# A two-layer mixer on one core: inputs and parameters laid out transposed, and the first modulation's depth tiles spread over the column groups

## The chip, the core and the metric

The kernel runs on one core of a Trainium2 chip. TensorE (PE) does the matrix products, VectorE (DVE) and ScalarE (ACT) the elementwise work, GpSimd (POOL) a few small powers, and SyncE (SP) issues all DMAs. The metric is the device time of one execution in microseconds. Three runs before the change took 1480.5 to 1486.15 us, median 1482.35.

## What is computed

Two layers of a mixer over 256 context tokens and 256 latent tokens, 2048 channels. What matters here, cut from the reference:

```python
def _modulation(cvec, ada_w, ada_b):
    m = jax.nn.silu(cvec) @ ada_w + ada_b      # (2048,) @ (2048, 3 * 2048)
    return jnp.split(m, 3, axis=-1)            # shift, scale, gate

def _layer(x, ctx, c, c_ctx, lp, cos, sin, update_ctx):
    sh_x, sc_x, g_x = [m[:, None, :] for m in _modulation(c, lp["ada_w"], lp["ada_b"])]
    sh_c, sc_c, g_c = _modulation(c_ctx, lp["ada_w"], lp["ada_b"])
    hx = rmsnorm(x, lp["pre_g"]) * (1.0 + sc_x) + sh_x
    hc = rmsnorm(ctx, lp["pre_g"]) * (1.0 + sc_c) + sh_c
    px = hx @ lp["w_in"]
    if update_ctx:
        pc = hc @ lp["w_in"]
    ...
    o_x = lax.map(lambda qs: _attend(qs[0], qs[1], k_nope, k_rope, v), ...)
    x_new = x + g_x * _branch_merge(o_x, px, lp)   # attention and long convolution, gated,
    ...                                            # normalised, times w_out
```

All is in float32. No projection of the first layer can start before its rows of `hx` are there, and these need the norm of x and the shift and scale of their channels, which need a (2 x 2048) by (2048 x 128) product for each tile of 128 channels.

## The kernel before

Activations lie with channels on the partitions: a tile is 128 channels by 512 tokens (256 of context, 256 latent), and the 16 tiles over the 2048 channels are "depth tiles". A float32 product is made of three passes with operands split into a high and a low part (`mm3`, two fp32r halves made by a ScalarE cast and a VectorE subtraction); the modulation matmuls alone run in plain float32, and each shows as two records in the trace.

The program is written by a list scheduler in Python (`Net`). Jobs yield operations; `run` issues, of those that could start first by its own estimate of every engine's queue (`start_of`, with the costs in `mm`, `act`, `dot` and so on), the one of the lowest rank. So the costs decide how jobs are interleaved on each engine. On top of that stands a fixed list of weight items (`items`, rank 10 on TensorE): `loader` loads them in order, `prepper` splits them, `products` multiplies them in order, each waiting for the names in its `need`. Buffers come from pools: slots of 256 KB (`s`), five of 512 KB (`raw`), two of 512 KB for high parts (`hi`). The loader takes raws when they are free and otherwise pairs of slots, if at least `SPARE_RAW` slots are to spare and the item is within `LOAD_DEPTH` of the current one.

The first stage goes so. `setup` and `load_x` load c, small tensors and x with tokens on partitions; `first_norm` transposes x on TensorE (64 transposes of 128x128, copied out of PSUM), squares it and makes the row factors. `params` transposes the per-channel parameters. Then come the blocks of channel tiles, `BLOCKS`: two of 2 tiles and three of 4. For a block, `ada_first` multiplies silu(c) (32 columns of `cs`, two of them used) by the scale columns and by the shift columns of the block. Each of the block's tiles has its own group of 32 columns of the array and accumulates over all 16 depth tiles:

```python
for c in range(n):                              # n = 2 or 4 tiles of the block
    o = (j * n + c) * P
    yield self.mm(ps[32 * c:32 * c + 32, 0:P], self.cs[:, kt, :], raws[0][:, o:o + P],
                  kt == 0, kt == KT - 1, ...)
```

`ada_cols` copies the sum, transposes it once and adds the bias; `hx_job` modulates the block's tiles of x; the projections' early items (`early`, seven groups, cut by depth into parts named `late`) use them. The list holds a block's modulation items, and from the ninth on (`EARLY_FROM`) the projection items of the block before between them. The first six projection items of the first block use two depth tiles only and are finished later (`by_depth`). The last four tiles of the shift are made on VectorE by dot products (`ada_slow`, `WAVE2`). After the first stage follow the other projections, attention heads, the long convolution and the output product of the first layer, then the second layer.

Names in the rows: `in_p_ada_first` are the first modulation's weights, `in_p_win` the input projection's, `cs` silu(c), `acc` and `mis` PSUM tiles (`acc` for items of the list, `mis` for everything else), `mcol` and `acol` shift and scale by channel. All matmuls are recorded at L232, transposes at L235, DMAs at L309, ScalarE's at L243 and L245, most of VectorE's at L250.

Of the kernel before, what the change touches and what calls it, by code (L numbers as in the profile page):

```python
# [9 lines left out]
F32 = mybir.dt.float32  # L10
# [23 lines left out]
N_SLOTS = 96 - 2 * (N_RAW + N_HI)  # L34
# [14 lines left out]
WAVE2 = (((0, 0, 12, 16),), ("ada0_0_4",), 4)  # L49
# [18 lines left out]
N_EARLY = 3  # L68
EARLY_FROM = 8
# [4 lines left out]
N_ROWS_A = sum(n for _, n in PARAM_ROWS)  # L74
N_ROWS_B = 96
# [94 lines left out]
class Net:  # L170
# [107 lines left out]
    def dot(self, junk, a, b, acc):  # L278
        return Op("dve", 0.07 + free_size(a) * 0.00104, [junk, acc], [a, b],
# [220 lines left out]
    def setup(self):  # L500
        nc, a, c = self.nc, self.a, self.const
        self.crow = c.tile([2 * KT, P], F32, name="crow")
        self.do(self.dma(self.crow, a["p_c"]))
        self.ident = c.tile([P, P], F32, name="ident")
        self.do(self.dma(self.ident, a["k_ident"]))
# [12 lines left out]
    def late_setup(self):  # L518
        a, c = self.a, self.const
        self.rows_a = self.slots.get()  # L520
        self.rows_b = self.slots.get()
        self.do(self.dma(self.rows_a[0:N_ROWS_A, 0:2 * P], a["p_rows_a"]))
        self.do(self.dma(self.rows_b[0:N_ROWS_B, 0:2 * P], a["p_rows_b"]))
# [4 lines left out]
    def cond(self):  # L528
        yield from self.on(self.crow, self.ident)
        (ps,) = yield from self.pget()  # L530
# [3 lines left out]
        self.mis.put(ps)  # L534
# [6 lines left out]
    def params(self):  # L541
        c = self.const
        self.par = []
        for l in range(2):
# [4 lines left out]
            d["col"] = c.tile([P, 224], F32, name=f"col_{l}")  # L549
            n = 0  # L550
            for k, m in PARAM_ROWS:
                d[k] = d["col"][:, n:n + m]
# [1283 lines left out]
```

## Time and profile before

| | |
|---|---|
| median of 3 runs | 1482.35 us (1480.5 to 1486.15) |
| span of the profiled execution | 1483.1 us |
| busy: PE, DVE, ACT | 98%, 80%, 47% |
| DMA | 328.92 MB, mean 222 GB/s |
| granted TensorE clock, mean | 0.995 |

The span runs from the first to the last instruction of one profiled execution. Busy times are shares of that span. A busy TensorE is not TensorE at its peak: records overlap, so throughput is read from the distance between starts or from the length of a row divided by its count, not from the mean duration of one.

### The profile page before, as it was taken

The page shows a single profiled execution, that of the slowest core. Times are in us where ns is not written, and L with a number is a line of the kernel's source. Part 1 is how long each engine was busy: PE and PEld are TensorE (multiplying, and loading weights), DVE is VectorE, ACT ScalarE, POOL GpSimd, SP SyncE. Part 2 cuts the span into 40 slices and gives each one's busy share as a digit, 9 for nine tenths or more (in the row PEclk, how much of TensorE's full clock was granted, in tenths as well). Part 3 has the DMA queues.
Part 4 walks back from the last instruction along what each step waited for, and adds up shares of the span by engine and source line. Part 5 has one row for each costly group of instructions (what it writes and reads, how often), then busy time and mean ns, then how long its engine had stood idle before and what let it go on. Part 6 is the DMA issues. An engine that isn't in the chain of part 4 may idle for free.

```text
span 1483.1 us, 26318 instructions
## 1 busy us (share of the span) xinstructions
PE 1457.0 (98%) x9700; PEld 1261.2 (85%) x9700; DVE 1190.2 (80%) x2522; ACT 692.6 (47%) x1339; POOL 16.4 (1%) x20
## 2 busy tenths in 40 slices
PE   7999999999999999999999999999999999999997
PEld 5677787778787777877778999999999989999997
DVE  5577999997888878998888988888868878786544
ACT  5421354335354452334334444566646666655542
POOL 0000000000000000000000000000000000000000
PEclk9999999999999999999999999999999999999999
DMA  9997875468466677566858886567728234668441
GB/s 324 356 334 239 286 263 205 159 212 308 151 195 215 223 250 251 170 228 220 299 191 301 296 281 196 167 227 260 245 89 310 90 113 133 234 201 288 164 143 57
DMA packets 165872, 328.92 MB, mean 222 GB/s; under 512 B 18501, under 2 KB 41068, under 8 KB 165744
## 3 DMA queue, kind: packets, MB, share of 16 engines
q1 hardware_dynamic: 165744, 327.25, 64.6%
q8 instruction: 76, 1.25, 0.3%
q14 instruction: 52, 0.43, 0.1%
HBM read 301.99 MB, written 25.18 MB: 221 GB/s over the span
## 4 chain that ended last, share of the span: by engine, by line
PE 88%; DMA 7%; DVE 2%; issue 1%; SPq 1%; ACT 1%; POOL 0%; DVEq 0%; POOLq 0%; ACTq 0%
PE acc L232 68%; PE mis L232 17%; PE mis L235 3%; DMA s<-in_p_ada_first 1%; DMA raw<-in_p_ada_first 1%; DMA s<-in_p_ada_slow 1%; DVE s L250 1%; DMA s<-in_p_win 1%; SPq L309 1%; DMA s<-in_ctx 1%; DVE junk L280 1%; DMA s<-in_p_uv 0%; DMA raw<-in_p_win 0%; DMA s<-in_p_ada_rest 0%; DMA h_d<-s 0%
## 5 line engine op out<-in xcount | busy, mean ns | idle before, releaser
L232 PE MATMUL acc<-s,hi 128*128 128x256 f32 (+1 forms) x2304 | 566.0, 337 | 0.5 <-ACT hi L243 0.4
L232 PE MATMUL acc<-s,s 128*128 128x256 f32 (+1 forms) x3216 | 489.4, 308 | 0.0
L232 PEld LDWEIGHTS acc<-s,s 128*128 128x128 f32 x3216 | 439.2, 191 | 30.5 <-issue 3.7
L232 PEld LDWEIGHTS acc<-s,hi 128*128 128x128 f32 x2304 | 388.4, 191 | 56.2 <-issue 11.5
L250 DVE TENSOR_TENSOR s<-s,s 128x512 fp32r<-128x512 f32 (+5 forms) x575 | 342.2, 623 | 42.3 <-ACT s L245 21.2
L232 PE MATMUL acc<-s,raw 128*128 128x256 f32 (+1 forms) x1104 | 371.1, 336 | 0.3 <-DVE raw L250 0.3
L280 DVE SCALAR_TENSOR_TENSOR junk<-s,s 128x512 bf16<-128x512 f32 x352 | 241.5, 686 | 26.9 <-DMA s<-crow_d 10.5
L232 PE MATMUL mis<-s,s 128*128 128x256 f32 (+2 forms) x1232 | 251.4, 341 | 1.2 <-ACT s L243 0.9
L232 PEld LDWEIGHTS acc<-s,raw 128*128 128x128 f32 x1104 | 210.3, 191 | 23.0 <-issue 2.5
L232 PEld LDWEIGHTS mis<-s,s 128*128 128x128 f32 (+1 forms) x1232 | 190.4, 189 | 43.9 <-issue 13.9
L243 ACT CAST s<-s 128x512 fp32r<-128x512 f32 (+3 forms) x324 | 180.3, 589 | 74.8 <-DVE s L250 28.5
L243 ACT CAST hi<-raw 128x1024 fp32r<-128x1024 f32 (+1 forms) x100 | 97.2, 972 | 121.4 <-PE acc L232 68.7
L250 DVE TENSOR_TENSOR raw<-raw,hi 128x1024 fp32r<-128x1024 f32 x88 | 107.3, 1220 | 19.7 <-ACT hi L243 19.1
L243 ACT CAST hi<-s 128x512 fp32r<-128x512 f32 x124 | 73.4, 618 | 92.9 <-PE acc L232 75.6
L250 DVE TENSOR_TENSOR raw<-s,hi 128x512 fp32r<-128x512 f32 x124 | 83.8, 686 | 34.4 <-ACT hi L243 33.4
L243 ACT COPY s<-mis 128x512 f32<-128x512 f32 (+3 forms) x101 | 48.6, 485 | 116.7 <-PE mis L232 90.5
L250 DVE TENSOR_TENSOR s<-mis,s 128x512 fp32r<-128x512 f32 (+2 forms) x128 | 84.6, 669 | 22.8 <-ACT s L243 17.3
L243 ACT CAST s<-mis 128x512 fp32r<-128x512 f32 (+1 forms) x100 | 56.6, 570 | 89.2 <-PE mis L235 48.3
L245 ACT ACTIVATE s<-acc 128x256 f32<-128x256 f32 (+1 forms) x88 | 37.5, 429 | 96.6 <-PE acc L232 81.2
L235 PE MATMUL mis<-ident,s 128*128 128x128 f32 (+1 forms) x369 | 66.8, 291 | 4.1 <-DMA s<-in_x 1.0
L250 DVE TENSOR_TENSOR s<-raw,s 128x512 fp32r<-128x512 f32 x106 | 69.8, 683 | 0.8 <-ACT s L243 0.7
L243 ACT CAST s<-raw 128x512 fp32r<-128x512 f32 x106 | 61.8, 617 | 9.1 <-DMA raw<-in_p_wout 6.2
(85 smaller groups left out, 916.9 us busy)
## 6 DMA issues: line engine op xcount, KB each, us to landing
s<-in_p_ada_slow SPq DMA_DIRECT2D x208, 256.0 KB, 3.3
raw<-in_p_win SPq DMA_DIRECT2D x99, 512.0 KB, 5.1
s<-in_p_win SPq DMA_DIRECT2D x178, 256.0 KB, 5.3
s<-in_p_wout SPq DMA_DIRECT2D x108, 256.0 KB, 4.9
raw<-in_p_wout SPq DMA_DIRECT2D x42, 512.0 KB, 3.8
s<-in_p_ada_first SPq DMA_DIRECT2D x62, 256.0 KB, 5.8
raw<-in_p_ada_first SPq DMA_DIRECT2D x25, 512.0 KB, 6.1
raw<-in_p_ada_rest SPq DMA_DIRECT2D x20, 512.0 KB, 4.7
```

The lines of the kernel that those rows point to most:

```text
L232: lambda: self.nc.tensor.matmul(out, lhsT, rhs, start=start, stop=stop), 0.2)
L235: return Op("pe", 0.11, [out], [in_], lambda: self.nc.tensor.transpose(out, in_, ident), 0.2)
L243: self.nc.scalar.copy(out, in_)
L245: self.nc.scalar.activation(out, in_, func, **kw)
L250: return Op("dve", fixed + n * rate, [out], ins, lambda: getattr(self.nc.vector, name)(out=out, **kw))
L280: lambda: self.nc.vector.scalar_tensor_tensor(out=junk, in0=a, scalar=1.0, in1=b, op0=ALU.mult, op1=ALU.mult, accum_out=acc))
L309: return Op("sp", n / 360e3, [dst], [src], lambda: self.nc.sync.dma_start(dst, src))
```

## The change

x and the context come in already transposed, as 16 tiles of 128 channels by 512 tokens, and so do c and the per-channel parameters; the transposes on TensorE, the copies and a DRAM copy of the transposed x go. The first norm squares tiles on ScalarE, adds them on VectorE and sums over the partitions by four small matmuls. In the first modulation, each group of 32 columns now takes every fourth depth tile and all columns of the block (256 or 512) at once; `ada_sum` copies the four partial sums, transposes them and adds them. An item is now 1 MB. The list of the first items is blended evenly: projections of the block before go between the modulation items from the first one. There are seven more slots, four early groups instead of three of the convolution's, a further reserve in the loader, and other costs in the scheduler.

```diff
-N_SLOTS = 96 - 2 * (N_RAW + N_HI)
+N_SLOTS = 103 - 2 * (N_RAW + N_HI)
-WAVE2 = (((0, 0, 12, 16),), ("ada0_0_4",), 4)
+WAVE2 = (((0, 0, 12, 16),), ("ada0_0_2",), 4)
-N_EARLY = 3
-EARLY_FROM = 8
+N_EARLY = 4
...
     def mm(self, out, lhsT, rhs, start=True, stop=True, share=1.0):
-            c = max(n, 480 if n < 256 else 0) / 2400 + 0.0025
+            c = max(n, 480 if n < 256 else 0) / 2400 + 0.0137
-            c = 4 * (n / 2400 + 0.0025) * share if n > 1 else 0.11
+            c = 4 * (n / 2400 + 0.003) * share if n > 1 else 0.11
     def dot(self, junk, a, b, acc):
-        return Op("dve", 0.07 + free_size(a) * 0.00104, [junk, acc], [a, b],
+        return Op("dve", 0.185 + free_size(a) * 0.00104, [junk, acc], [a, b],
+    def promised(self):
+        return max((k.want for k in self.pending if k.name.startswith("mod0")), default=0)
...
     def cond(self):
-        yield self.tr(ps[:, 0:32], self.crow, self.ident[0:32, 0:32])
-        for s in range(2):
-            yield self.act(self.cs[:, :, s], ps[:, s * KT:(s + 1) * KT], AF.Silu)
+        yield self.act(self.cs[:, :, 0:2], self.ccol.rearrange("p (k s) -> p k s", s=2), AF.Silu)
...
     def ada_first(self, sec, t0, t1):
-        n = t1 - t0
-        deep = 8 // n
-        for i in range(2 * n):
+        n = (t1 - t0) * P
+        deep = 2048 // n
+        for i in range(KT // deep):
             def load(raws, i=i):
-                yield from self.load(raws[0], self.a["p_ada_first"][sec, 2 * t0 + i])
+                for h in range(2):
+                    yield from self.load(raws[h], self.a["p_ada_first"][sec, 2 * t0 + 2 * i + h])
             def pe(raws, i=i):
                 for j in range(deep):
-                    kt = deep * i + j
-                    for c in range(n):
-                        o = (j * n + c) * P
-                        yield self.mm(ps[32 * c:32 * c + 32, 0:P], self.cs[:, kt, :], raws[0][:, o:o + P],
-                                      kt == 0, kt == KT - 1, share=0.34 if n == 4 else 0.55)
+                    kt, c = deep * i + j, j % 4
+                    h, o = divmod(j * n, 1024)
+                    yield self.mm(ps[32 * c:32 * c + 32, 0:n], self.cs[:, kt, :], raws[h][:, o:o + n],
+                                  kt < 4, kt >= KT - 4, share=0.37)
+    def ada_sum(self, l, sec, acc, t0, t1):
+        yield self.act(g[:, 0:n], acc[:, 0:n])
+        for i in range(t1 - t0):
+            yield self.tr(ps[:, i * P:(i + 1) * P], g[:, i * P:(i + 1) * P], self.ident)
+        v = ps[:, 0:n].rearrange("p (t c r) -> p t r c", c=4, r=32)[:, :, 0:2]
+        yield self.vsum(m, v)
...
     def load_x(self):
+        for kt in range(KT):
+            t = self.slots.get()
+            self.do(self.dma(t, self.a["p_xt"][kt]))
     def first_norm(self):
+        for kt in range(KT):
+            yield from self.on(self.xt[kt])
+            yield from self.sumsq(sq, self.xt[kt], T)
+        self.bc0 = yield from self.rstd_bc([(sq, T)], D)
     def hx_job(self, t0, t1):
             yield from self.modulate(0, kt, self.xt[kt], self.bc0, hx[kt], ((0, slice(0, L)), (1, slice(L, T))))
+            self.slots.put(self.xt[kt])
-            for kt in range(KT):
-                yield self.dma(self.xt_d[kt], self.xt[kt])
-                self.slots.put(self.xt[kt])
     def loader(self):
-                return it.halves and i <= self.at + LOAD_DEPTH and self.spare() >= SPARE_RAW
+                return it.halves and i <= self.at + LOAD_DEPTH and self.spare() >= SPARE_RAW + self.promised()
...
     def build(self):
-            w = late[n - 1] if n else []
-            ...
-                while k < len(w) and i >= EARLY_FROM and \
-                        (k + 1) * (len(ada) - EARLY_FROM) <= (i + 1 - EARLY_FROM) * len(w):
+            items += self.blend(ada, late[n - 1] if n else [])
```

What this does to the order of the instructions is seen at three places. First the DMA queue (SP) before the first projection weights (`in_p_win`), before the change:

```order
L309 DMA s_63_440<-in_p_ada_first 128x512
L309 DMA raw_6_461<-in_p_ada_first 128x1024
L309 DMA raw_7_467<-in_p_ada_first 128x1024
L309 DMA raw_8_486<-in_p_ada_first 128x1024
L309 DMA s_66_500<-in_p_win 128x512
L309 DMA s_67_501<-in_p_win 128x512
```

Sixteen items of 512 KB stood ahead of the first weights. The same place of the queue after the change:

```order
L307 DMA s_47_284<-in_p_ada_first 128x512
L307 DMA s_48_285<-in_p_ada_first 128x512
L307 DMA s_55_311<-in_filt_w 64x512
L307 DMA s_53_307<-in_p_win 128x512
L307 DMA s_54_308<-in_p_win 128x512
L307 DMA s_56_327<-in_p_win 128x512
L307 DMA s_57_328<-in_p_win 128x512
L307 DMA raw_5_338<-in_p_ada_first 128x1024
```

Five items of 1 MB stand ahead now (four whole loads and twelve halves), then two projection tiles, and the sixth modulation item follows them. On TensorE, the end of the modulation items ahead of the first projection (`acc_1`), before:

```order
L232 MATMUL mis_28_604<-raw_6_461,cs 32x128 x8
L232 MATMUL mis_28_604<-raw_7_467,cs 32x128 x8
L232 MATMUL mis_28_604<-raw_8_486,cs 32x128 x8
L235 MATMUL mis_30_664<-ident,s_93_657 128x64
L232 MATMUL acc_1_674<-s_76_549,s_94_658 128x512
L232 MATMUL acc_1_674<-s_77_550,s_94_658 128x512
```

Both blocks of two tiles were finished, the transpose of the last column sum included. The same place on TensorE after the change:

```order
L230 MATMUL mis_6_355<-s_42_269,cs 32x256 x2
L230 MATMUL mis_8_392<-s_45_282,cs 32x256 x2
L233 MATMUL mis_9_395<-ident,s_64_393 128x128 x2
L230 MATMUL mis_8_392<-s_46_283,cs 32x256 x2
L230 MATMUL mis_8_392<-s_47_284,cs 32x256 x2
L230 MATMUL mis_8_392<-s_48_285,cs 32x256 x2
L230 MATMUL acc_1_457<-s_67_407,s_79_435 128x512
L230 MATMUL acc_1_457<-s_68_408,s_79_435 128x512
```

Only the first item of the second block (`mis_8`) stands ahead of the first projection; two transposes belong to a sum. On TensorE in the first block of four tiles (`mis_33` before, `mis_17` after), a piece of before:

```order
L232 MATMUL mis_33_860<-s_92_643,cs 32x128 x4
L232 MATMUL mis_33_860<-raw_11_666,cs 32x128 x8
L232 MATMUL mis_33_860<-raw_12_672,cs 32x128 x8
L232 MATMUL mis_33_860<-s_110_703,cs 32x128 x4
L232 MATMUL mis_33_860<-s_111_704,cs 32x128 x4
L232 MATMUL mis_33_860<-s_128_808,cs 32x128 x4
```

Eight modulation items stood in a row. The piece after the change:

```order
L230 MATMUL acc_20_812<-s_136_673,s_110_559 128x512
L230 MATMUL mis_17_842<-s_144_756,cs 32x512
L230 MATMUL mis_17_842<-s_145_757,cs 32x512
L230 MATMUL mis_17_842<-s_146_758,cs 32x512
L230 MATMUL mis_17_842<-s_147_759,cs 32x512
L230 MATMUL acc_21_849<-s_133_670,s_114_579 128x512
```

One item of four matmuls stands between the products of two projection tiles.

## Rows read from the trace of the kernel before

**Rows 1.** The page, part 1: busy time, share of the span and instructions.
```profile
PE 1457.0 (98%) x9700; PEld 1261.2 (85%) x9700; DVE 1190.2 (80%) x2522; ACT 692.6 (47%) x1339; POOL 16.4 (1%) x20
```
**Rows 2.** Stretches: length, busy time and count by engine, clock, DMA share, GB/s.
```profile
core 0: us, PE busy (x) PEld busy (x) DVE busy (x) ACT busy (x) POOL busy (x), PEclk, DMA share, GB/s
20.00:40.00 20.00, 17.40 (x238) 13.70 (x240) 9.22 (x31) 8.70 (x22) 1.02 (x1) 1.00 1.03 381
68.00:72.00 4.00, 4.00 (x14) 1.32 (x12) 0.94 (x5) 0.59 (x1) 0.00 (x0) 0.57 0.98 359
72.00:150.00 78.00, 77.89 (x619) 56.23 (x619) 57.72 (x122) 16.78 (x30) 0.00 (x0) 1.00 0.86 293
160.00:164.00 4.00, 4.00 (x11) 3.10 (x10) 3.96 (x11) 3.18 (x5) 0.00 (x0) 0.50 1.02 414
200.00:1476.00 1276.00, 1272.40 (x8216) 1123.95 (x8214) 1044.10 (x2197) 620.75 (x1189) 14.49 (x13) 1.00 0.61 208
```
**Rows 3.** The chain that ended last, first 150 us: start, us, what.
```profile
34.78 8.04 DMA s<-in_p_win
...
62.04 4.75 DMA raw<-in_p_ada_first
```
**Rows 4.** DMA issues: tiles, engine, count, KB each, median us to landing.
```profile
s<-in_p_ada_first SPq DMA_DIRECT2D x62, 256.0 KB, 5.8
raw<-in_p_ada_first SPq DMA_DIRECT2D x25, 512.0 KB, 6.1
```
**Rows 5.** Timeline of TensorE: start, us, what, count, [idle before and its releaser].
```profile
43.88 11.16 PE L232 MATMUL acc<-s,s 128*128 128x512 f32 x48
...
61.34 0.64 PE L232 MATMUL mis<-raw,cs 128*32 128x128 f32 x16
...
67.76 0.73 PE L232 MATMUL mis<-raw,cs 128*32 128x128 f32 x10
68.42 3.68 PE L232 MATMUL mis<-s,dft 128*128 128x512 f32 x4
...
92.76 0.64 PE L232 MATMUL mis<-raw,cs 128*32 128x128 f32 x16
93.33 3.06 PE L232 MATMUL acc<-s,s 128*128 128x512 f32 x12
...
99.06 1.95 PE L232 MATMUL mis<-s,cs 128*32 128x128 f32 x64
...
150.43 1.52 PE L232 MATMUL mis<-s,cs 128*32 128x128 f32 x48
...
157.44 0.65 PE L232 MATMUL mis<-s,cs 128*32 128x128 f32 x8 [1.06 <-DMA s<-in_p_ada_first]
158.48 0.47 PE L235 MATMUL mis<-ident,s 128*128 128x128 f32 x1 [0.39 <-ACT s L243]
159.40 1.22 PE L232 MATMUL acc<-s,hi 128*128 128x512 f32 x2 [0.44 <-ACT hi L243]
...
312.28 1.06 PE L232 MATMUL mis<-raw,cs 128*32 128x512 f32 x8
313.27 0.74 PE L232 MATMUL acc<-s,hi 128*128 128x512 f32 x2
...
578.75 0.74 PE L235 MATMUL mis<-ident,s 128*128 128x128 f32 x4
```
**Rows 6.** Timeline of VectorE around the first modulated tiles.
```profile
33.41 1.66 DVE L250 SCALAR_TENSOR_TENSOR s<-s,acol,s 128x256 f32<-128x256 f32 x4
35.00 1.66 DVE L250 SCALAR_TENSOR_TENSOR s<-s,mcol,s 128x256 fp32r<-128x256 f32 x4
...
43.49 0.69 DVE L250 TENSOR_TENSOR s<-s,s 128x512 fp32r<-128x512 f32 x1 [3.96 <-ACT s L243]
```
**Rows 7.** Timeline of ScalarE at the same place.
```profile
33.92 1.71 ACT L245 ACTIVATE s<-s,mcol 128x256 fp32r<-128x256 f32 x4 [0.42 <-DVE s L250]
```
**Rows 8.** Waits of TensorE from 200 us to the end, the longest in total.
```profile
PE mis L232 <- ACT s L243: 0.9, 1, 0.9
```

More of the change, by code (lines that the diff above doesn't have):

```diff
@@ L73 @@
               ("grp_g_mla", 8), ("grp_g_hy", 8))
-N_ROWS_A = sum(n for _, n in PARAM_ROWS)
-N_ROWS_B = 96
+N_COL = 224
 G_Q, G_KV, G_HY, G_GM, G_GH = 0, 2, 3, 15, 19
@@ L501, in setup @@
         nc, a, c = self.nc, self.a, self.const
[L502 to L505, printed above, removed]
+        self.ccol = c.tile([P, 2 * KT], F32, name="ccol")
+        self.do(self.dma(self.ccol, a["p_ccol"]))
         self.zt = c.tile([33, L], F32, name="zt")
@@ L583, in pe @@
                 for j in range(deep):
-                    kt = deep * i + j
-                    for c in range(n):
-                        o = (j * n + c) * P
-                        yield self.mm(ps[32 * c:32 * c + 32, 0:P], self.cs[:, kt, :], raws[0][:, o:o + P],
-                                      kt == 0, kt == KT - 1, share=0.34 if n == 4 else 0.55)
+                    kt, c = deep * i + j, j % 4
+                    h, o = divmod(j * n, 1024)
+                    yield self.mm(ps[32 * c:32 * c + 32, 0:n], self.cs[:, kt, :], raws[h][:, o:o + n],
+                                  kt < 4, kt >= KT - 4, share=0.37)
             def post(i=i):
-                if i == 2 * n - 1:
-                    self.job(f"ada0_{sec}_{t0}", self.ada_cols(0, sec, hold["ps"], ((t0, t1),)), want=1,
+                if deep * (i + 1) == KT:
+                    self.job(f"ada0_{sec}_{t0}", self.ada_sum(0, sec, hold["ps"], t0, t1), want=1,
                              after=("params",), rank=1)
-            out.append(Item(load, None, pe, post, need=("cond",) if i == 0 else (), halves=True))
+            out.append(Item(load, None, pe, post, need=("cond",) if i == 0 else (), nraw=2, halves=True))
         return out
+    def ada_sum(self, l, sec, acc, t0, t1):
+        p = self.par[l]
+        (g,) = yield from self.sget()
+        n = (t1 - t0) * P
+        yield self.act(g[:, 0:n], acc[:, 0:n])
+        self.mis.put(acc)
+        yield from self.on(g)
+        (ps,) = yield from self.pget()
+        for i in range(t1 - t0):
+            yield self.tr(ps[:, i * P:(i + 1) * P], g[:, i * P:(i + 1) * P], self.ident)
+        self.slots.put(g)
+        v = ps[:, 0:n].rearrange("p (t c r) -> p t r c", c=4, r=32)[:, :, 0:2]
+        m = p["mcol"][:, sec, t0:t1]
+        yield self.vsum(m, v)
+        self.mis.put(ps)
+        r = slice(sec * KT + t0, sec * KT + t1)
+        yield self.tt(m, m, p["ada_b"][:, r].unsqueeze(2).broadcast_to([P, t1 - t0, 2]), ALU.add)
+        if sec == 1:
+            yield self.stt(p["acol"][:, t0:t1], m, 1.0,
+                           p["pre_g"][:, t0:t1].unsqueeze(2).broadcast_to([P, t1 - t0, 2]), ALU.add, ALU.mult)
     def ada_cols(self, l, sec, acc, parts):
@@ L1611, in layer_jobs, with blend @@
         self.job(f"ysb{l}", self.y_split(l, 1, nq), after=(f"y{l}_1",), want=9 if nq == T else 1)
+    def blend(self, a, b):
+        out, k = [], 0
+        for i, it in enumerate(a):
+            out.append(it)
+            while k < len(b) and k < (i + 1) * len(b) / len(a):
+                out.append(b[k])
+                k += 1
+        return out + b[k:]
     def then(self, item, f):
@@ L1669, in build @@
         self.then(main[-1], drop_hx0)
-        k = 0
-        for i, it in enumerate(main):
-            items.append(it)
-            while k < len(side) and k < (i + 1) * len(side) / len(main):
-                items.append(side[k])
-                k += 1
+        items += self.blend(main, side)
         for s in (1, 0):
```

92 lines of the change are left out of this document (23 added, 69 removed).

## Prediction

> **What bounds the kernel now.** I read the share of busy time first, then the table of stretches, then the chain of waits and the timelines of the first 165 us. TensorE is busy 98% of the span [rows 1]. The table of stretches says where the rest is: from 200 to 1476 us it is busy for 1272.4 of 1276 us, from 72 to 150 us for 77.89 of 78 [rows 2]. So the large part of the run is TensorE's own work, and waiting is found in two places only. One is the start: the stream of projection matmuls (48 in a row) begins at 43.88 us [rows 5], and the chain of waits reaches it through a weight tile issued at 34.78 us that lands 8.04 us later, at 42.82 [rows 3]. While it waits the DMA engines are full: 381 GB/s from 20 to 40 us [rows 2]. The start is bound by bytes in the order of the queue. The other place is two runs of modulation items without projections between them, at 61 and at 150 us. There TensorE eats 512 KB in about half a microsecond, faster than they come, so it waits, and behind each run stands a stretch at a low clock: 0.57 granted from 68 to 72 us, 0.50 from 160 to 164 (0.50 is 1.2 GHz, 1.00 is 2.4 GHz) [rows 2].
>
> **The start.** What is queued ahead of the first half of the first weight tile: before, 16 modulation loads of 512 KB (8192 KB), after, the four whole 512 KB loads and 12 halves of 256 KB that stand there in the new order (5120 KB; sizes in [rows 4]). The x and context tiles are 4096 KB both times. Small tensors: 42 KB more by the shapes of the new parameter tile, the second copy of c and the rows that go. That is 3030 KB or 3.10 MB less, 8.1 us at 381 GB/s: the tile lands at 42.82 - 8.1 = 34.7 us. Now something else is late: the first two modulated tiles. The loads of the first block stand behind the same bytes as before, so its columns are ready as before, plus about 0.2 us for the added sum over the four groups. Before, VectorE's first pass started at 33.41 us and its second (the low parts) took 35.00 to 36.66 [rows 6]; the ScalarE pass between them ended at 35.63 [rows 7]. After, the low part of the weight tile stands behind three of the four low parts: 33.6 + 1.66 + 1.25 = 36.5, and 0.69 for itself makes 37.2 us. Before, that same operand was ready at 43.49 + 0.69 = 44.18 [rows 6]. The stream starts 7.0 us earlier (bounds: 9.2 if the tile alone decided, 0 if one more chain came late). **-7.0**
>
> But fewer modulation items lie ahead of it. Before, both two-tile blocks were finished by then; now three of the four items of the second block come after the start. An item holds 8 matmuls of 256 columns, a width the trace does not show. Bounds: two 128-column matmuls, 0.57 us per 8 of these with four groups (16 records from 92.76 to 93.33), so 1.14; or half of a 512-column one, 8 records in 0.99 us (312.28 to 313.27), so 0.99 [rows 5]. If the groups did not overlap, it would be some four times as much. I take 1.07, near both. Each change to 32-column matmuls and back costs too: 12 projection matmuls after such an item take 3.06 us against 12 x 0.2325 = 2.79 in the long row [rows 5]; 0.25. So 3 x 1.32. **+3.9** (bounds 3 and 13)
>
> **The large blocks.** Blocks of four tiles held 40 items, now 20 of double size. Before, 16 stood alone (0.57 + 0.25) and 24 in runs (1.95 us for 64 records, 0.49 per item): 13.1 + 11.8 + 0.7 for three changes = 25.6 us. After, 20 x (0.99 + 0.25) = 24.8. **-0.8**. The column sums are new: 24 transposes stand in the stream, 5 blocks of four and two pairs, where 6 did before. Four take 0.74 us [rows 5], so 5 x 0.5 + 2 x 0.25 less 0.6 for those that go; bounds 1 and 4. **+2.1**
>
> **The clock at the start.** Before, 64 transposes of x and 256 records of modulation matmuls kept TensorE occupied until 43 us. Now the transposes are gone and up to 36 us there are only some 32 matmuls of 256 columns in small bursts. The trace shows what thinness did twice: behind the first run of modulation items the granted clock was 0.57 over 4 us, 1.7 us lost, behind the second 0.50, 2.0 us lost [rows 2]. I charge one such stretch at the head of the stream, where nothing hides it (bounds 0 and 3.7). **+1.8**. The Trainium skill (TensorE: Matmul & The Clock Gate, "What's actually happening") says that the throttled clock is the default and that activity lifts it, so that a cold array begins at 1.2 GHz. By that rule the head of the new stream is slow, which speaks against the change; by the one row of full clock from 20 to 40 us, carried over, it would not be, and the sum would be 1.8 us lower.
>
> **The two runs.** The new order puts one or two projection tiles behind every modulation item. What goes: the eight rows from 61.34 to 67.76 us hold 152 records, at 0.0305 us 4.6 us, and last until 68.42, so 2.4 are waits; the nine rows from 150.43 to 157.44 hold 128 (3.9 us) and last until 158.48, so 4.1; then 0.83 of waits at 158 to 159 us for the columns [rows 5]; and the two slow-clock stretches 1.7 and 2.0 [rows 2]. Together **-11.0** (bounds 0 and -11.0). The new pairing can be fed: an item and a full tile need 1.5 MB, 4.1 us at 381 GB/s, and hold TensorE for 1.24 + 24 x 0.2325 = 6.8; with the half tiles at first it is 1 MB or 2.8 us against 4.0. What was held up before at 62.04 us was a load that waited for a buffer [rows 3]; there are now seven more of 256 KB, and each x tile is given back as soon as it is modulated instead of at the end. Late next is the modulated input of the next block: behind the last item of a block stand a copy, transposes, a sum and the first tile's modulation (some 4 us), and before them on TensorE half a tile (2.8) and an item (1.2). I charge **+1.0** for it in all (bounds 0 and 6).
>
> **What costs nothing.** The squares of x stay on ScalarE; 15 additions of about 0.6 us take the place of PSUM copies on VectorE, all long before the first block's loads are in. The 16 stores of x and their issue go at a place where TensorE is busy without a gap. The fourth early group adds six additions (4 us) to VectorE, which is busy for 57.72 of 78 us there [rows 2]; without that cover it costs up to 4 us. The earlier dot products lie on the same cover. The new cost constants move side jobs against each other over the whole kernel; from 200 us on TensorE idles 3.6 us in all, of which 0.9 for its longest named wait [rows 2, 8], so they can give at most that and cost what the second rival says. I take 0.
>
> **Sum**: -7.0 + 3.9 - 0.8 + 2.1 + 1.8 - 11.0 + 1.0 = -10.0 us. The profiled execution has a span of 1483.1 us; the median of the runs shown is 1482.35, so the execution is typical. 1482.35 - 10.0 = 1472 us. Half a per cent, 7.4 us, is about what a measurement of this kernel can tell from no change, so faster means under 1474.9 and slower over 1489.8.
>
> **Rivals.**
> (a) The waits stay, elsewhere. All the modulation bytes are still needed within the first stage, a doubled item takes four 256 KB buffers at once where two were enough, and the loader now keeps nine more buffers free until the last modulation starts, so it prefetches less. If the 11.0 us of waits return, 1482.35 + 1.0 = 1483 us: no change. Against it: from 72 to 150 us, where items already alternate with tiles, TensorE idles 0.11 us [rows 2]. Halfway, 1478.
> (b) Slower: waits behind the attention heads. The list is re-sorted by other constants, and the softmax's transposes or products could come due on TensorE before ScalarE and VectorE have their operands, with the projections queued behind them. The price of one is the row: 0.9 us [rows 8]. There are 24 chains (two for each of 8 heads in the first layer, one in the second). All of them late cost 21.6 us: 1494. From 20 such waits on the kernel is slower by more than half a per cent. For it: VectorE is busy for 1044 of the 1276 us there [rows 2], so there is little slack. Against it: only a handful of waits are seen now, and the new constant for a 512-column matmul, 0.227 us, is nearer to the 0.2325 of [rows 5] than the old 0.216.
> (c) Slower: the 32-column items do not keep the clock up. Each now lasts 1 us, and if each of 23 cost a slow stretch of 1.7 us, it would be 39 us: 1511; it decides from 11 on. Against it: the modulation items of that same width at 312 us leave no mark, projections behind them go on at 0.74 us for two [rows 5].
>
> **Chances.** The forecast 0.65 (its own range 1465 to 1479, of which 0.55 under 1474.9), (a) 0.20, (b) 0.10, (c) 0.05. So faster 0.55, same 0.10 + 0.20 = 0.30, slower 0.15. The range reaches from 1464 (the start bound by bytes alone 2.2, the clock full 1.8, no new waits 1.0, and most of the 3.6 us of idle time after 200 us) to 1484, which takes in (a); left out are (b), (c) and a little below.
>
> **What would show it.** First projection matmul near 37 us, at about 0.43 us each for a few microseconds; items of 1 us alternating with projections; no wait over 1 us on a modulation load between 40 and 170 us; full clock after the head; the stretch from 200 us to the last matmul as long as before but shifted by 10 us. Wrong: a first matmul after 41 us, waits for modulation loads or modulated tiles over 5 us, or TensorE idling more than 10 us after 200 us.

## The result, and the profile after

The changed kernel takes 1491.61 us (median of 4 runs, 1491.1 to 1492.81) against 1481.42 for the kernel before (4 runs). The ratio is 1.0074, with a 95% interval of 1.0051 to 1.0097: slower by 10 us, where 10 us faster was forecast. The profiled execution took 1492.81 us, its span is 1491.0.

The page of the changed kernel, part 1, is read beside [rows 1]:

```profile
PE 1445.6 (97%) x9050; PEld 1230.7 (83%) x9050; DVE 1195.7 (80%) x2552; ACT 693.4 (47%) x1349; POOL 14.1 (1%) x20
```

TensorE is busy for 11.4 us less and the span is 7.9 us longer: the work went, and waits took more than its place. The table of stretches says where (columns as in [rows 2]; first the changed kernel, then the kernel before in the same later stretches):

```profile
20.00:40.00 20.00, 17.41 (x118) 9.86 (x119) 8.62 (x22) 8.16 (x16) 1.02 (x1) 1.00 1.04 375
44.00:200.00 156.00, 149.50 (x705) 98.80 (x703) 111.32 (x235) 45.76 (x85) 0.00 (x0) 0.98 0.84 293
102.00:106.00 4.00, 4.00 (x12) 2.83 (x10) 4.00 (x11) 2.21 (x5) 0.00 (x0) 0.57 1.02 364
163.00:167.00 4.00, 3.74 (x10) 2.98 (x11) 4.00 (x11) 2.74 (x6) 0.00 (x0) 0.63 0.04 14
200.00:700.00 500.00, 492.13 (x2335) 379.22 (x2335) 439.13 (x953) 225.43 (x412) 4.91 (x4) 1.00 0.61 205
700.00:1400.00 700.00, 697.29 (x5180) 657.05 (x5179) 578.25 (x1234) 367.28 (x730) 6.76 (x8) 1.00 0.64 216
```

```profile
44.00:200.00 156.00, 150.67 (x1149) 111.81 (x1150) 122.64 (x266) 49.90 (x94) 0.00 (x0) 0.97 0.87 305
200.00:700.00 500.00, 498.99 (x2363) 389.22 (x2362) 439.16 (x948) 220.40 (x383) 3.90 (x3) 1.00 0.64 213
700.00:1400.00 700.00, 698.24 (x5230) 659.76 (x5229) 570.13 (x1190) 372.13 (x738) 10.05 (x9) 1.00 0.64 217
```

From 200 to 700 us TensorE idles 7.87 us where it idled 1.01. From 44 to 200 it idles 6.5 where it idled 5.3, although the waits of the two runs were to go there. The timeline of TensorE in the changed kernel (columns as in [rows 5]) shows the start and what stands in the place of the runs:

```profile
25.66 1.94 PE L230 MATMUL mis<-raw,cs 128*32 128x256 f32 x16
27.36 0.67 PE L230 MATMUL mis<-s,cs 128*32 128x256 f32 x4
...
28.45 2.18 PE L230 MATMUL mis<-s,cs 128*32 128x256 f32 x32
...
34.76 5.99 PE L230 MATMUL acc<-s,s 128*128 128x512 f32 x24 [1.12 <-ACT s L241]
...
45.31 1.07 PE L230 MATMUL mis<-s,cs 128*32 128x256 f32 x16
46.31 5.78 PE L230 MATMUL acc<-s,s 128*128 128x512 f32 x24
...
92.23 1.06 PE L230 MATMUL mis<-s,cs 128*32 128x512 f32 x8
...
94.66 0.60 PE L233 MATMUL mis<-ident,s 128*128 128x128 f32 x4
...
97.43 1.07 PE L230 MATMUL mis<-s,cs 128*32 128x512 f32 x8
99.38 0.50 PE L230 MATMUL acc<-s,s 128*128 128x512 f32 x1 [0.88 <-ACT s L243]
101.62 7.21 PE L230 MATMUL acc<-s,s 128*128 128x512 f32 x23 [1.74 <-DVE s L248]
...
159.67 1.06 PE L230 MATMUL mis<-s,cs 128*32 128x512 f32 x8
161.62 0.50 PE L230 MATMUL acc<-s,hi 128*128 128x512 f32 x1 [0.88 <-ACT s L243]
163.26 0.50 PE L230 MATMUL acc<-s,hi 128*128 128x512 f32 x1 [1.14 <-DVE s L248]
```

The stream starts at 34.76 us, 9.1 earlier than in [rows 5]. The modulation items alternate with projection tiles and wait for no load. But at 99 and at 161 us the first tile of the next block waits twice, for the high and the low part of its modulated input; and at each place a stretch of low clock follows the second wait (0.57 and 0.63 granted in the table above, 23 matmuls in 7.21 us where the long row of [rows 5] would take 5.3).

The low clock itself cost little at the first place. In g1, a kernel of the experiments below that has the same order on TensorE up to 161 us, the clock stays at 1.00 there, and TensorE waits a third time for VectorE instead:

```profile
34.88 7.58 PE L230 MATMUL acc<-s,s 128*128 128x512 f32 x24 [1.82 <-ACT s L241]
...
102.13 3.00 PE L230 MATMUL acc<-s,s 128*128 128x512 f32 x12 [1.75 <-DVE s L248]
106.51 2.79 PE L230 MATMUL acc<-s,s 128*128 128x512 f32 x11 [1.38 <-DVE s L248]
```

The 23 matmuls from 102.13 us on end 7.17 us after their start, against 7.21 with the low clock. So it is the late input that counts. (The row at 34.88 us is used further down.) The timelines of VectorE and, below it, of ScalarE at this place in the changed kernel show why it is late:

```profile
95.46 0.18 DVE L287 TENSOR_REDUCE mcol<-mis 128x8 f32<-128x32 f32 x1
...
96.26 1.66 DVE L248 SCALAR_TENSOR_TENSOR s<-s,acol,s 128x256 f32<-128x256 f32 x4
97.85 1.40 DVE L248 TENSOR_TENSOR s<-s,mis 128x512 f32<-128x512 f32 x2
99.16 1.22 DVE L248 TENSOR_TENSOR raw<-raw,hi 128x1024 fp32r<-128x1024 f32 x1
100.30 1.67 DVE L248 SCALAR_TENSOR_TENSOR s<-s,mcol,s 128x256 fp32r<-128x256 f32 x4
```

```profile
97.54 0.59 ACT L241 COPY s<-acc 128x512 f32<-128x512 f32 x1 [2.18 <-PE acc L230]
98.02 1.71 ACT L243 ACTIVATE s<-s,mcol 128x256 fp32r<-128x256 f32 x4
```

The block's last item ends at 93.3 us. After ScalarE's copy its transposes stand behind two matmuls of the filter and start at 94.66, the sum follows at 95.46, the first pass of the modulation at 96.26. ScalarE's pass (the high part) could follow from 96.7, when the first piece is there, but in its queue stands the copy of a projection's result that is ready only at 97.54; it starts at 98.02, and TensorE waits the first time. The second pass of VectorE (the low part) could follow ScalarE's first piece from 98.5, but VectorE takes two filter additions and a weight split first (97.85 to 100.30), and TensorE gets the operand at 101.6.

The waits of TensorE by cause (total, times, longest), changed kernel, 44 to 200 us and then 200 to 1400, the costliest of each:

```profile
PE acc L230 <- DVE s L248: 3.4, 3, 1.7
PE acc L230 <- ACT s L243: 1.8, 2, 0.9
```

```profile
PE mis L233 <- DMA s<-u_d: 1.7, 3, 0.7
PE mis L230 <- ACT s L241: 1.7, 2, 1.5
PE mis L230 <- DVE s L248: 1.6, 4, 0.7
PE mis L233 <- DVE s L265: 1.5, 2, 1.1
PE mis L233 <- ACT s L243: 1.1, 1, 1.1
PE acc L230 <- DVE raw L248: 1.0, 1, 1.0
```

After 200 us nothing stands out: 16 waits, none above 1.5 us, none for a weight load, most of them of transposes and side products (`mis`) that TensorE reaches before VectorE, ScalarE or a DMA has their operand. In [rows 8] the longest cause had one wait of 0.9.

To compare kernels that do the same work in another order I count as "loss" of a stretch its length less the sum of its TensorE records, each at the pitch of its shape in undisturbed rows (0.2283 us for a 128x512 matmul, 0.120 for 128x256, and so on). It holds a fixed part, since some pairs of shapes never reach that pitch; only differences say something. By this count the changed kernel has 1401.9 us of work against 1410.8, 8.9 less. By the work that is left at a time it is 5.7 us ahead at 44 us and 4.6 at 200, then 1.6 behind at 400, 5.8 behind at 700 and 7.8 behind at the end. One pitch is a choice: the 896 records of 128-column modulation matmuls, which only the kernel before has, stand at 0.0356 us (0.57 for 16 in [rows 5]). At the 0.0305 of its long row (1.95 for 64) they are 4.6 us less, and the changed kernel is 2.5 us ahead at 44 us; the lead at 200 us and all that comes later stay. So two things are to be explained: why the lead at 200 us is 4.6 and not 10, and the 12.4 us lost after it.

### The profile page after: what moved, and what is told of

It is laid out like the page before. It is cut to its first block, busy times and chain, and to the rows that moved or that the text cites. A ratio compares the mean times of both kernels' runs of the same rounds, so it can differ in the third digit from the quotient of the medians.

```text
span 1491.0 us, 25074 instructions
## 1 busy us (share of the span) xinstructions
PE 1445.6 (97%) x9050; PEld 1230.7 (83%) x9050; DVE 1195.7 (80%) x2552; ACT 693.4 (47%) x1349; POOL 14.1 (1%) x20
## 4 chain that ended last, share of the span: by engine, by line
PE 73%; DMA 11%; DVE 9%; issue 2%; ACT 2%; SPq 2%; DVEq 0%; POOLq 0%; POOL 0%; ACTq 0%
PE acc L230 56%; PE mis L230 15%; DVE s L248 7%; PE mis L233 2%; SPq L307 2%; DMA s<-in_p_ada_first 2%; DMA s<-in_p_win 1%; DMA s<-in_p_ada_slow 1%; DMA raw<-in_p_win 1%; DVE raw L248 1%; ACT s L241 1%; DVE junk L278 1%; DMA s<-u_d 1%; DMA s<-in_p_ada_rest 1%; DMA s<-in_p_xt 1%
## 5 line engine op out<-in xcount | busy, mean ns | idle before, releaser
L230 PE MATMUL acc<-s,s 128*128 128x256 f32 (+1 forms) x3648 | 577.3, 313 | 4.5 <-DVE s L248 2.5
L230 PEld LDWEIGHTS acc<-s,s 128*128 128x128 f32 x3648 | 506.3, 191 | 56.4 <-DVE s L248 8.1
L230 PE MATMUL acc<-s,hi 128*128 128x256 f32 (+1 forms) x2016 | 491.9, 335 | 2.0 <-DVE s L248 1.1
L230 PEld LDWEIGHTS acc<-s,hi 128*128 128x128 f32 x2016 | 339.3, 190 | 57.2 <-issue 13.1
L230 PE MATMUL acc<-s,raw 128*128 128x256 f32 (+1 forms) x960 | 320.3, 334 | 1.0 <-DVE raw L248 1.0
L230 PE MATMUL mis<-s,s 128*128 128x256 f32 (+3 forms) x1232 | 252.2, 344 | 3.5 <-ACT s L241 1.9
L241 ACT CAST hi<-raw 128x1024 fp32r<-128x1024 f32 (+1 forms) x70 | 65.6, 939 | 107.5 <-PE acc L230 79.7
L241 ACT COPY s<-mis 128x512 f32<-128x512 f32 (+1 forms) x96 | 48.0, 500 | 134.9 <-PE mis L230 107.0
L248 DVE TENSOR_TENSOR raw<-raw,hi 128x1024 fp32r<-128x1024 f32 x58 | 70.7, 1219 | 20.6 <-ACT hi L241 19.7
L248 DVE TENSOR_TENSOR s<-s,acc 128x512 f32<-128x512 f32 (+1 forms) x59 | 38.7, 673 | 31.8 <-PE acc L230 31.8
```

The lines of the kernel that those rows point to most:

```text
L230: lambda: self.nc.tensor.matmul(out, lhsT, rhs, start=start, stop=stop), 0.2)
L241: self.nc.scalar.copy(out, in_)
L248: return Op("dve", fixed + n * rate, [out], ins, lambda: getattr(self.nc.vector, name)(out=out, **kw))
```

## The experiments

Losses are those of the profiled execution, in us, which lies up to 5 us off the median (f2 3.9 below it, e4 4.8 above); times are medians; ratios are against the kernel before, run on the same chip, with their 95% interval.

| run | time | ratio | loss 0 to 44 | 44 to 200 | from 200 |
|---|---|---|---|---|---|
| before | 1481.4 | | 24.4 | 14.2 | 25.7 |
| changed | 1491.6 | 1.0051 to 1.0097 | 27.6 | 15.5 | 38.1 |
| e1 changed, old costs | 1491.8 | 1.0055 to 1.0089 | 27.8 | 14.7 | 38.2 |
| e2 before, new costs | 1500.7 | 1.0109 to 1.0143 | 24.8 | 16.6 | 42.9 |
| e3 changed, three early | 1500.1 | 1.0103 to 1.0139 | 28.6 | 21.8 | 33.8 |
| e4 changed, dots later | 1505.0 | 1.0142 to 1.0181 | 28.6 | 23.2 | 45.6 |
| f1 before, 0.3 ns | 1489.9 | 1.0046 to 1.0081 | 24.4 | 12.0 | 32.0 |
| f2 before, dot 0.08 | 1486.1 | 1.0025 to 1.0048 | 24.2 | 8.5 | 28.7 |
| f3 changed, 0.3 ns | 1492.9 | 1.0057 to 1.0102 | 27.8 | 15.9 | 39.8 |
| f4 changed, lag 0.6 | 1560.9 | 1.0518 to 1.0558 | 32.3 | 29.8 | 89.8 |
| g1 changed, dots and filter earlier | 1491.5 | 1.0046 to 1.0076 | 28.7 | 15.4 | 36.2 |
| g2 changed, dots earlier | 1493.3 | 1.0060 to 1.0102 | 29.2 | 14.1 | 36.3 |
| g3 changed, old order | 1490.8 | 1.0039 to 1.0075 | 32.1 | 13.7 | 32.7 |
| g4 before, new order | 1508.1 | 1.0151 to 1.0192 | 24.3 | 25.8 | 39.8 |
| h1 changed, half dots | 1496.7 | 1.0077 to 1.0134 | 27.8 | 14.2 | 40.5 |
| h2 before, half dots | 1486.0 | 1.0018 to 1.0046 | 24.8 | 14.4 | 28.9 |
| h3 changed, one section on TensorE | 1512.0 | 1.0175 to 1.0221 | 28.9 | 13.7 | 38.0 |
| i1 changed, wide dots | 1491.7 | 1.0053 to 1.0107 | 27.6 | 13.3 | 36.5 |
| j1 changed, old order and costs | 1482.6 | 1.0001 to 1.0020 | 31.6 | 15.5 | 22.2 |
| j2 before, new layout | 1477.0 | 0.9963 to 0.9984 | 32.1 | 3.8 | 30.7 |

**The parts one at a time.** e1 takes four cost constants back, e2 puts them alone into the kernel before (two of the four are shown; the share that `ada_first` gives its matmuls stays with the layout in both):

```diff
-            c = max(n, 480 if n < 256 else 0) / 2400 + 0.0137
+            c = max(n, 480 if n < 256 else 0) / 2400 + 0.0025
-        return Op("dve", 0.185 + free_size(a) * 0.00104, [junk, acc], [a, b],
+        return Op("dve", 0.07 + free_size(a) * 0.00104, [junk, acc], [a, b],
```

> The changed kernel with the five cost constants of the list as they were before (0.0025 per matmul, 0.0025 and share 0.27 for the 32-column ones of the other items, 0.07 for a dot product). Theory A (the new constants make the list place the side jobs' transposes and products on TensorE just in time, so TensorE waits for their operands; this is the 10.4 us lost between 200 and 700 us): about 1481, and TensorE busy again for over 99.5% from 200 to 700 us. Theory B (the fourth early group and the earlier dot products load VectorE): 1490 to 1492. Theory C (the buffers kept free for the modulation jobs starve the loader): 1490 to 1492.

> The kernel before with only the five new cost constants. Theory A: slower than before by 8 to 12 us, 1490 to 1494, with waits of TensorE for ScalarE and VectorE between 200 and 700 us. Theories B and C: 1480 to 1484, no new waits.

e2 is 19 us slower than before: the constants alone do cost more than the whole change. The costliest waits of its TensorE from 200 us on are again side jobs that come due too early:

```profile
PE mis L232 <- DVE s L250: 3.7, 6, 2.4
PE mis L232 <- ACT s L243: 3.6, 5, 1.4
PE mis L235 <- DMA s<-u_d: 1.8, 3, 1.1
PE mis L235 <- DVE s L267: 1.4, 1, 1.4
```

But e1, which takes them back, wins nothing: it waits less from 500 to 700 us and more around 260 and after 1000. So theory A in its simple form falls. Theory C (the buffers kept free) had 1490 to 1492 for e1, as measured, but 1480 to 1484 for e2; the loader's reserve and the seven more slots were never taken back by themselves.

e3 (`N_EARLY = 3`) and e4 (the dots of the last shift tiles released by `ada0_0_4`) undo two other parts:

> The changed kernel with three early groups instead of four. Theory A: 1490 to 1492, the waits after 200 us stay. Theory B: 1483 to 1487, as six additions of 0.7 us and the partial sums of one group go from VectorE and the waits for modulated tiles at 99 to 110 us with them. Theory C: 1490 to 1492.

> The changed kernel with the dot products of the last four shift tiles released by the third block's columns again, not by the second's. Theory A: 1487 to 1490, at most the 4.4 us that were lost between 100 and 120 us come back. Theory B: 1483 to 1487. Theory C: 1490 to 1492.

Both are slower than the changed kernel, by 8 and 13 us. None of the three theories had that. Theory B falls.

**Chance of the interleaving.** Theory D was formed on this: any edit of a cost or a rank makes the list interleave all side jobs anew, and the kernel before is a good draw.

```diff
-            c = max(n, 480 if n < 256 else 0) / 2400 + 0.0025
+            c = max(n, 480 if n < 256 else 0) / 2400 + 0.0028
```

> The kernel before with one cost constant moved by 0.3 ns (0.0025 to 0.0028 per fp32r matmul): the work is the same, the interleaving is drawn anew. Theory D (any redraw of the list's interleaving loses 5 to 20 us against the kernel before, whose order happens to wait for 2.8 us only between 200 and 1400 us): 1487 to 1502, with 8 to 15 us of waits. Theory A (the size of the constant matters, as it places TensorE's side jobs just in time): 1480 to 1485, since 0.3 ns is a fortieth of the change's step.

> The kernel before with the dot product's cost at 0.08 instead of 0.07. Theory D: 1487 to 1502. Theory A: 1480 to 1485.

> The changed kernel with 0.0140 instead of 0.0137 per fp32r matmul. Theory D: a new draw, 1487 to 1503, whichever way, and where it differs from the changed kernel it does so by waits at other places. Theory A: 1490 to 1493, as the changed kernel.

> The changed kernel with the results of VectorE and ScalarE counted as visible 0.6 us after their end instead of 0.15, so that the list places TensorE's dependent side jobs later. Theory A, in the form that the list leaves no margin for the real delays: TensorE idles less than 4 us between 200 and 1400 us, 1482 to 1486. Theory D: one more draw, 1487 to 1503.

f1 costs 9.9 us for 0.3 ns. Its TensorE is busy for 491.27 of the 500 us from 200 to 700:

```profile
200.00:700.00 500.00, 491.27 (x2335) 383.69 (x2334) 432.73 (x923) 218.59 (x382) 5.91 (x3) 1.00 0.61 207
```

f2 costs 5 to 6 us, just under D's range and above A's; f3 is the changed kernel again within its scatter, which both theories had. So a neutral edit costs 1 to 10 us in these three, and D may be a large part. f4 shows that a margin written into the list is no cure: with results counted as late by 0.6 us, TensorE idles 51.5 us from 700 to 1400 us, and neither theory had its 1560.9.

**VectorE.** In the changed kernel VectorE is busy only 111.32 us from 44 to 200 (122.64 before); the fall is at 140 to 200 us, where its waits for projections to finish come to 24.4 us:

```profile
DVE s L248 <- PE acc L230: 24.4, 8, 4.1
```

By the sum of its later records it has 1196 us of work left at 200 us, against 1179 in the kernel before. Theory F blamed this. g1 and g2 release side work into the gap (`hx0_8` for `hx0_12`), g3 and g4 swap the order of the first stage's items:

```diff
-            items += self.blend(ada, late[n - 1] if n else [])
+            w = late[n - 1] if n else []
+            k = 0
+            for i, it in enumerate(ada):
+                items.append(it)
+                while k < len(w) and i >= 4 and (k + 1) * (len(ada) - 4) <= (i + 1 - 4) * len(w):
+                    items.append(w[k])
+                    k += 1
+            items += w[k:]
```

> The changed kernel with the second layer's dot products and filters released after the fourth block (hx0_8) instead of the last (hx0_12). Theory F (in the new order the last block's columns come 24 us later, VectorE idles 24 us between 150 and 200 us because nothing else is released, and the 17 us of VectorE work that it is then behind make TensorE wait until 700 us): the hole from 170 to 200 us fills, VectorE has about 1180 us left at 200 us instead of 1196, and the time is 1480 to 1485. Theory D (any redraw of the interleaving loses, wherever VectorE stands): 1487 to 1503.

> The same with the dot products alone released after the fourth block, the second filter as in the changed kernel. Theory F: the dot products fill the hole as well, 1480 to 1486. Theory D: 1487 to 1503, and no relation between it and the run before.

> The changed kernel with the old placing of the first stage's items: a block's first half of modulation items stands alone, the projection tiles stand among the second half (from the fourth item on, since items are twice as large). Theory F: the modulation comes as early as before, VectorE has 1176 to 1185 us left at 200 us, the waits for modulation loads come back (4 to 8 us between 50 and 170 us), and less than 4 us of waits stand between 200 and 700: 1478 to 1485. Theory D: 1487 to 1503.

> The kernel before with the new placing of the first stage's items alone. Theory F: the waits of the two runs go (12 us in all until 200 us), VectorE has 10 to 17 us more left at 200 us than before (1190 to 1196), and the time is 1484 to 1492, as what is won early is paid back by 700 us. Theory D: 1487 to 1502. The prediction's mechanism, with no cost elsewhere: 1470 to 1474.

In g1 to g3 VectorE has 1186, 1188 and 1182 us left at 200 us, as F wanted, and the times do not move. g4 says that the new order by itself is dear in the kernel before: 26 us. The waits between 44 and 200 us are the first part (TensorE busy for 144.12 of 156; by cause 6.7 us for operands of the filter's matmuls and 4.9 for modulated tiles), and its VectorE is idler still:

```profile
44.00:200.00 156.00, 144.12 (x1153) 105.33 (x1152) 105.56 (x229) 37.24 (x72) 0.00 (x0) 0.96 0.80 281
200.00:700.00 500.00, 492.14 (x2338) 382.01 (x2337) 431.21 (x935) 215.30 (x380) 3.53 (x3) 0.99 0.63 208
```

Over the runs so far, e2 aside, the loss from 200 us on still rose with the VectorE work left (25.7 us at 1179 left, 45.6 at 1203 in e4), so F2 said that the load itself is what counts. Four kernels take load away; h1 and h2 sum half of each dot product only (`w[:, 0:256]`), i1 makes 160 products of 1024 elements of the 320 of 512, h3 drops `WAVE1`:

> The changed kernel with every dot product over 256 instead of 512 elements; it leaves out half of each sum. VectorE has some 60 to 80 us less to do after 200 us. Theory F2 (what TensorE loses after 200 us grows with the VectorE work that is left then, about 0.6 us for each us, whatever put it there): the loss after 200 us falls from 38 us to the level of the kernel before or under it (20 to 26 by the same count), the time is 1472 to 1479. Theory D (each redraw loses by chance): 1487 to 1503.

> The kernel before with every dot product over 256 elements; it leaves out half of each sum. Theory F2: the kernel before is near the floor already, 1477 to 1482, and the changed kernel with the same cut is 3 to 8 us faster than this one, since its lead of 4.6 us at 200 us is kept. Theory D: 1485 to 1500.

> The changed kernel with half as many dot products, each over 1024 elements, in four buffers of 512 KB of their own (slots 95 instead of 103). The whole computation. VectorE saves the fixed cost of 160 products, some 35 us. Theory F2: the loss after 200 us falls by 10 to 16 us, 1475 to 1482. Theory D: 1487 to 1503.

> The changed kernel with one of the second layer's three modulation sections (128 dot products, 98 us of VectorE) made by TensorE in 16 more items of the list (8 us of matmuls) instead of VectorE. Theory F2: 8 to 12 us more of TensorE's work, 12 to 16 us less lost after 200 us: 1484 to 1491. Theory D: 1496 to 1512.

The dot products between 200 and 1000 us, in the changed kernel, in h1 and in i1 (operation, tiles, shapes, count, busy us, mean ns):

```profile
L278 DVE SCALAR_TENSOR_TENSOR junk<-s,s 128x512 bf16<-128x512 f32 x320 | 219.6, 686 | 19.1 <-DMA s<-in_p_ada_slow 8.0 <-DMA s<-crow_d 7.0
```

```profile
L278 DVE SCALAR_TENSOR_TENSOR junk<-s,s 128x256 bf16<-128x256 f32 x320 | 134.8, 421 | 56.2 <-DMA s<-in_p_ada_slow 34.0 <-DMA s<-crow_d 15.3 <-issue 1.9
```

```profile
L280 DVE SCALAR_TENSOR_TENSOR junk<-wide,wide 128x1024 bf16<-128x1024 f32 x160 | 194.9, 1218 | 11.9 <-DMA wide<-in_p_ada_slow 9.0 <-DMA wide<-crow_d 1.5
```

VectorE lost 85 us of work in h1 and 38 in i1 (there with the reads of the sums), and neither is faster than the changed kernel. h2, with the same cut in the kernel before, is 5 us slower than the kernel before. h3 takes 98 us away, adds 16 us to TensorE by the count, and is 20 us slower, with the loss from 200 us on unchanged (38.0). F2 falls: VectorE's load does not decide.

**Two parts taken back at once.** Theory G: order and costs each suffice for the loss, so both must go. j1 is the changed kernel with both old. j2 goes on and takes back the fourth early group, the earlier dots, the seven buffers and the loader's reserve; the layout, the wider modulation items and what goes with them remain.

> The changed kernel with both the old placing of the first stage's items and the old cost constants. Theory G (the new order and the new costs each suffice to cost 12 to 17 us after 200 us, as they did alone in the kernel before, so that taking back one of them brings nothing): the loss after 200 us falls to 26 to 30 us from 38, the lead at 200 us stays near 2 to 5 us, 1476 to 1482. Theory D (no part is the cause; every draw of the interleaving is dearer than the order of the kernel before): the loss after 200 us stays at 32 to 40, 1486 to 1500.

> The kernel before with the transposed layout and the 256- and 512-column modulation items alone: old costs, old placing, three early groups, dots released by the third block, 96 slots, no reserve for the modulation jobs. Theory G: 1476 to 1482, the same or a little faster than before, as TensorE has 8.9 us less to do. Theory D: 1486 to 1500 although the work is less.

j1 comes out at 1482.58, 9 us under the changed kernel and level with the kernel before, although TensorE has less to do; its loss from 200 us on is 22.2, the lowest of all. Both figures lie just outside what G said (1476 to 1482, 26 to 30) and far from D's. j2 takes 1476.96 us, 4.0 less than before, and is the fastest kernel here. The rows are the two stretches from 44 to 700 us, first of j1, then of j2:

```profile
44.00:200.00 156.00, 149.43 (x683) 100.21 (x684) 126.09 (x277) 48.73 (x91) 0.00 (x0) 0.98 0.87 299
200.00:700.00 500.00, 496.31 (x2377) 389.28 (x2376) 441.06 (x947) 223.99 (x409) 7.77 (x4) 1.00 0.63 209
```

```profile
44.00:200.00 156.00, 154.18 (x735) 108.96 (x736) 132.15 (x287) 52.71 (x99) 0.00 (x0) 1.00 0.87 308
200.00:700.00 500.00, 492.27 (x2351) 384.79 (x2353) 437.41 (x940) 216.42 (x379) 3.90 (x3) 1.00 0.61 205
```

They win at different places. From 44 to 200 us j1 waits as much as the changed kernel, and little afterwards; j2 loses almost nothing from 44 to 200 us (3.8) and then 30.7. Neither has the early start. The stream of projection matmuls starts at 43.11 us in j1 and at 43.84 in j2, as in the kernel before, while g4, the kernel before with the new order, starts its first projection at 35.90 (the rows are of j2, then of g4):

```profile
43.84 11.51 PE L230 MATMUL acc<-s,s 128*128 128x512 f32 x48
```

```profile
35.90 0.49 PE L232 MATMUL acc<-s,s 128*128 128x512 f32 x1 [1.81 <-ACT s L245]
```

So the early start belongs to the new order and not to the layout, and the fastest kernel here does without it. That the two kernels with old order and old costs are the fastest of the 17 that do the whole work with an edit (15 others at 1486 to 1561) speaks for G over mere chance. But j2's later loss (30.7) is above the kernel before's, and with up to 10 us for a neutral edit no single step between two of these kernels, such as the 9 us from the changed kernel to j1 or the 5.6 from j1 to j2, can be put down to its part.

## Why the prediction was wrong

- **The start, -7.0 and +3.9.** Right in kind: the stream starts at 34.76 us, 9.1 earlier and 2.4 before the 37.2 of the text; a modulation item of 256 columns takes 1.00 us (45.31 to 46.31), 1.07 was taken. The lead at 44 us is 5.7 (2.5 at the other pitch), where the two terms give 3.1.
- **The cold clock, +1.8.** Right in mechanism and nearly in size; that the profiled execution shows no low clock at the head is luck of that execution. There the first 24 projection matmuls take 5.9 us. In the traces of the ten other kernels that start in the same order (e1, e3, e4, f3, f4, g1, g2, h1, h3, i1) the granted clock falls to 0.50 between 33.8 and 36.0 us, and the same 24 take 7.1 to 7.6 us (12.0 in f4; the row of g1 at 34.88 us stands above). Before that the array was slow in the changed kernel too: 16 records of 256-column modulation matmuls take 1.70 us from 25.66 us on (the next row starts at 27.36), 32 take 2.18 from 28.45 on, and 16 take 1.00 from 45.31 on. So the 1.00 that the table shows for 20 to 40 us does not hold before some 27 us. The rule that the Trainium skill gives (TensorE: Matmul & The Clock Gate, "What's actually happening"), a throttled clock until activity lifts it, agrees with these rows.
- **The two runs, -11.0, and the late modulated tiles, +1.0.** The first step that failed. The waits for modulation loads went, but waits for the modulated tiles came in their place (5.2 us named, over the 5 that the prediction gave as a sign of being wrong), and in this execution the two stretches of low clock that were booked as gone came back behind them. The clock is not what decides: g1, g2, h1 and h3 have the full clock from 44 to 200 us and lose 13.7 to 15.4 there. In the changed kernel the loss from 44 to 200 us is 15.5 against 14.2: the two terms together are worth +1.3 (-1.7 at the other pitch), not -10.0. Rival (a) had the outcome, waits that stay elsewhere, but for loads and buffers. The size that failed is the chain behind a block's last item: some 4 us were put down for copy, transposes, sum and modulation, with 4.0 us of TensorE work as cover. Measured, it is 8.3 us from the item's end (93.3) to the operand (101.6), since other work stands in the chain on TensorE, ScalarE and VectorE, and the cover was 5.2 (93.3 to 98.5).
- **"The new cost constants ... I take 0."** The second step that failed. The bound was wrong in kind: the 3.6 us of idle time after 200 us limits a gain, and the loss was left to rival (b), at 0.10. The constants alone cost 19 us in the kernel before, although 0.227 us is nearer to the measured 0.2325. From 200 to 1400 us the changed kernel idles 10.6 us where 2.8 was idle, and loses 12.4 by the count, in waits of 0.2 to 1.5 us spread over side jobs of all kinds: rival (b)'s mechanism, with its mark (TensorE idling over 10 us after 200 us), though not behind the attention heads alone. Taking the constants back alone does not undo it, and the order alone takes 5.4 of the loss and nothing of the time; with both back it is 22.2, in one trace, and the time is that of the kernel before. So the step that failed is shown, a redraw priced at nothing; which part of it costs is not.
- **The order of the first stage** was counted for what it does up to 165 us only. The early start comes from it alone (g3, the changed kernel with the old order, starts at 43.5 us). That an edit of this list redraws everything behind it (0.3 ns cost 9.9 us in the kernel before, about 1 in the changed one) was in no term; alone in the kernel before, the new order lost 11.6 us up to 200 us and 14 after.
- **The fourth early group and the earlier dots** at nothing: alone in reverse they make the changed kernel 8 and 13 us slower, so nothing shows that they cost there.
- **Two slips.** 5 x 0.5 + 2 x 0.25 - 0.6 is 2.4 and not 2.1, and the 0.39 us of idle time before 158.48 us stand both in the 4.1 and in the 0.83. Neither matters beside a miss of 20 us.
- **Sum.** By the losses: -8.9 of work, +3.2 up to 44 us (TensorE idles there instead of doing the work that went), +1.3 to 200 us, +12.4 after it: +8.0, where the spans differ by 7.9. The medians differ by 10.2. In other words, the changed kernel is 4.6 us ahead at 200 us where 10 were forecast, and loses 12.4 after that where nothing was.

What stays open: why the list made with constants nearer to the chip's leaves TensorE waiting more often. It was not shown whether that is a rule or the draw.

## What to carry to other kernels

Where a list scheduler sets the order, an edit of a cost, a rank or an item's place redraws the whole program behind it; find out first what a neutral edit costs (here 1 to 10 us of 1480), and do not price any part more finely than that. Change the data layout first with the old order and the old costs, and time that alone: here it is the one version that is faster, by 4.0 us, which is less than a neutral edit can cost, so that it is not shown to be the layout's own worth. Idle time that is left bounds what a redraw can win, never what it can cost.

## What was not expected of the hardware

- Instructions in the same order get the low clock in one execution and not in another. In the changed kernel TensorE did one modulation item and one matmul between 97.43 and 101.62 us, with waits of 0.88 and 1.74 us, and from 102 to 106 us the granted clock was 0.57. In g1, with the same order on TensorE and waits of 0.88 and 1.75 us, it was 1.00 there; but at the head of the stream, from 34 to 44 us, it was 0.83 in g1 and 1.00 in the changed kernel.
- A low clock in front of a late operand can be free: 23 matmuls took 7.21 us with it and 7.17 without, as they had to wait for VectorE in either case.
- A VectorE dot product of 512 elements takes 686 ns, of 256 elements 421, of 1024 elements 1218, and 81 ns for each read of its sum: some 155 ns of each are fixed, so joining two saves 0.24 us; here that was worth nothing, as VectorE did not bound the kernel.
